# Computing the norm factors as a power of -0.5 on GpSimd, in one encoder layer kernel

## The chip, the cores and the metric

The kernel runs on one core of a Trainium2 chip. The core has five engines that run their own queues of instructions and meet by semaphores: TensorE (PE, with its weight loads PEld), VectorE (DVE), ScalarE (ACT), GpSimd (POOL) and SyncE (SP), which issues the transfers between memory and the on-chip buffers. The metric is the time of one execution on the device, in microseconds (us); the kernel before takes 1599.53 us as the median of three runs (1599.46 to 1602.58).

## The reference, cut to what matters

The model is one encoder layer on two sequences (a prompt and a sample) of 512 tokens with width 1024, each with a memory of 256 rows. All arithmetic is in 32-bit floats. The part that matters here is the norm:

```python
def _rmsnorm(x, g):
    xf = x.astype(jnp.float32)
    y = xf * lax.rsqrt(jnp.mean(xf * xf, axis=-1, keepdims=True) + EPS)
    return (y * g.astype(jnp.float32)).astype(x.dtype)
```

It is used on the input of the layer, on the memory, on the output of each of the four differential attention heads, on the input of the feed-forward part, and on the final output:

```python
    xn = _rmsnorm(x, p['norm_mix'][l])
    mn = _rmsnorm(mem, p['norm_mem'][l])
    h = xn @ p['w_in'][l]
    ...
    merged = term if merged is None else merged + term
    x = x + merged @ p['w_out'][l]
    xn2 = _rmsnorm(x, p['norm_ffn'][l])
    gate, up = jnp.split(xn2 @ p['w_ffn_in'][l], 2, axis=-1)
    return x + (jax.nn.silu(gate) * up) @ p['w_ffn_out'][l]
```

Between them lie a state space branch (S5) with a scan over the tokens, a differential attention of four heads, a cross attention to the memory, and gates that merge the three branches. Their functions on ScalarE are exponentials (softmax), hyperbolic tangents (the gates, GELU and SiLU) and squares.

## The kernel before

Activations are kept transposed: 128 features on the partitions, 512 tokens of a sequence along the free dimension. A product is a chain of matmuls with 128x128 weights and 512 columns that adds up in a bank of PSUM. To hold 32-bit precision each operand is split into a high and a low part (`split`, lines 134 and 135: ScalarE rounds, VectorE subtracts), and each product takes three matmuls (`mm3`). So TensorE has the most work of the engines.

The stages follow each other: norm of the inputs and memory products (to about 50 us of the profile), the S5 branch with gate products set between (to about 360 us), cross attention (to about 490 us), differential attention (to about 770 us), merging and the output projection (to about 940 us), the first feed-forward product in a form with seven products in place of eight (to about 1345 us), the second one, and the final norm.

A norm goes through one helper, `factor`. It gets the sums of squares of a sequence with tokens on the partitions, in a tile of 128x4 (`ss`, in PSUM or SBUF). ScalarE takes the root of the mean plus epsilon (line 198, Sqrt with scale and bias), VectorE the reciprocal (line 199), and then four transposes on TensorE with a broadcast operand (through line 69) spread the factors over all partitions, in a bank of PSUM named `bktr`, of which there are two to four. Later instructions of VectorE multiply the data with that bank. The calls are these, sixteen in all:

- two for the input (`ss0`, `ss1`), and one for the memory, all in the first 360 us;
- eight in `normed`, one for each head and sequence of the differential attention, with a bias of zero, since epsilon is added to the sums at line 896 already;
- two through `rstd` for the norm ahead of the feed-forward part, in the first round of its loop (`i == 0`);
- three in `final`, at the end of the kernel.

What sets the order: all instructions of an engine run in the order of its queue. In most of the kernel that order is made by a planner, which lays out the instructions by its own estimate of their durations (`schedule_with_timeline_sim=True`) and follows the order of the program where it has no reason to differ. `issue_after` puts instructions behind a named one on the same engine. In the cross attention, the differential attention, the last round of the first feed-forward product and nearly all of the second one, `PE.on = True` keeps TensorE's instructions in the order of the program; the other engines are planned there too. There `fill(n)` writes n matmuls of other work from a queue between the parts of the attention, so that TensorE has something to do while the other engines work. The loop of the differential attention handles one tile of 128 queries a step; `squares` of a head and sequence stands at the end of one step and `normed` at the end of the next, with two `fill(10)` and the transposes of the softmax between:

```python
        fill(10)
        if 1 < i <= n + 1 and steps[i - 2][2] == 3:
            squares(i - 2)
        if i > 2 and steps[i - 3][2] == 3:
            normed(i - 3)
```

GpSimd works in this kernel on adds and multiplies of SBUF tiles: the rotary embedding of queries and keys (lines 755 and 756), sums of weights (lines 454 to 457, 1023 to 1026), sums of squares (line 182), and products of the feed-forward part (line 1166).

Of the kernel before, what the change touches and what calls it, by code (L numbers as in the profile page):

```python
# [10 lines left out]
F32 = mybir.dt.float32  # L11
F32R = mybir.dt.float32r
I32 = mybir.dt.int32
AF = mybir.ActivationFunctionType
ALU = mybir.AluOpType
# [4 lines left out]
P = 128  # L20
L = 512
DM = 1024
# [3 lines left out]
EPS = 1e-6  # L26
# [46 lines left out]
def encoder(ctx: ExitStack, tc: tile.TileContext, a, out):  # L73
    nc = tc.nc
    V, S, PO, PE = nc.vector, nc.scalar, nc.gpsimd, InOrder(tc, nc.tensor)
# [3 lines left out]
    cst = ctx.enter_context(tc.tile_pool(name="cst", bufs=1))  # L79
# [32 lines left out]
    def aux():  # L112
        return bank("tr")
# [4 lines left out]
    nc.sync.dma_start(vec, a["vecs"])  # L118
    onec = cst.tile([P, 2], F32, name="onec")
    V.memset(onec, 1.0)  # L120
    V.memset(cst.tile([P, 8], F32, name="pad_l"), 0.0)
    epsc = cst.tile([P, 1], F32, name="epsc")
    S.activation(out=epsc, in_=onec[:, 0:1], func=AF.Sqrt)
    S.activation(out=epsc, in_=onec[:, 0:1], func=AF.Copy, scale=EPS)
# [1 line left out]
    def vcol(name, i=0):  # L126
        o = VEC[name][0] + i
        return vec[:, o : o + 1]
# [55 lines left out]
    def new_acc():  # L184
        return rp.tile([P, L], F32, tag="acc", name="acc", bufs=2)

    def rstd(acc, n, nt=4):


        ss = aux()  # L190
        for t in range(nt):
            PE.matmul(ss[:, t : t + 1], acc[:, t * P : (t + 1) * P], onec[:, 0:1], start=(t == 0), stop=(t == nt - 1))
        return factor(ss, n, nt)

    def factor(ss, n, nt=4, bias=epsc):

        rs = rp.tile([P, 4], F32, tag="rs", name="rs", bufs=4)
        S.activation(out=rs[:, :nt], in_=ss[:, :nt], func=AF.Sqrt, scale=1.0 / n, bias=bias)
        V.reciprocal(rs[:, :nt], rs[:, :nt])
        bc = aux()  # L200
        for t in range(nt):
            PE.transpose(bc[:, t * P : (t + 1) * P], rs[:, t : t + 1].broadcast_to([P, P]), ident)
        return rs, bc
# [26 lines left out]
    def sums(src, tag="wb", ss=None, ts=range(4)):  # L230

        nonlocal last_sq
        if ss is None:
            ss = rp.tile([P, 4], F32, tag="ss", name="ss", bufs=3)
        for t in ts:
            tk = slot(tag, [P, DM], name="tk")
            nc.sync.dma_start(tk, src[t])
            last_sq = S.activation(out=tk, in_=tk, func=AF.Square, accum_out=ss[:, t : t + 1])
        return ss
# [90 lines left out]
    with queued():  # L330
        x_load(0, range(3))
    norm = []
    mem_k(2, mw[2], lambda: norm.append(factor(ss0, DM)[1]))
    mw.append(weight(a["w_mv"][0]))
    with queued():
# [14 lines left out]
    with yielding(last_s):  # L350
        x_norm(0, norm[0], range(5, 8))
        _, bc = factor(ss1, DM)
# [163 lines left out]
    with behind():  # L516
# [3 lines left out]
        rs_, bc = factor(sums(a["memN"], "ld"), DM)  # L520
# [170 lines left out]
    for i in range(-AHEAD, len(steps) + 1):  # L691
        if i + AHEAD < len(steps):
            h, s, lt = steps[i + AHEAD]
# [12 lines left out]
        if 0 <= i < len(steps):  # L706
            h, s, lt = steps[i]
# [8 lines left out]
        if i > 0 and steps[i - 1][2] == 3:  # L716
            h, s, _ = steps[i - 1]
# [112 lines left out]
    s0, ss, osb = {}, {}, {}  # L830
# [66 lines left out]

    def normed(i):
        h, s, _ = steps[i]
        _, bc = factor(ss[h, s], P, bias=0.0)  # L900
        V.scalar_tensor_tensor(out=osb[h, s], in0=osb[h, s], scalar=g04, in1=bc, op0=ALU.mult, op1=ALU.mult)
        nc.sync.dma_start(bD[1, h, :, s * L : (s + 1) * L], osb[h, s])

    n = len(steps)
    for i in range(-1, n + 3):
        if i % 2 and i + 1 < n:
            scores(i + 1)
        if i == 22:
            queue.insert(1, first_in())
        fill(10 if i < n - 1 else 16)  # L910
        if 0 <= i < n:
            turn(i)
        if 0 < i <= n and steps[i - 1][2] % 2:
            outputs(i - 1)
# [5 lines that stand above are left out]
# [215 lines left out]
    for i in range(KFF):  # L1135
# [16 lines left out]
        if i == 0:  # L1152
            for s in range(NS):
                _, bc = rstd(accs[s], DM)
# [159 lines left out]
    def final(ss, c0, n, ready=(), late=()):  # L1314

        cs = slice(c0, c0 + n)
        _, bc = factor(ss, DM, n // P)
        if ready:
            b_ = new_acc()
            S.copy(b_[:, :n], bc[:, :n])  # L1320
        for m in (0, 1, 4, 5, 6, 7, 2, 3) if late else range(KD):
            if m in ready:
                PO.tensor_tensor(out=y[m][:, cs], in0=y[m][:, cs], in1=b_[:, :n], op=ALU.mult)
            else:
                with ExitStack() as es_:
                    if m in late:
                        es_.enter_context(tc.issue_after(last_add.ins))
                    V.scalar_tensor_tensor(out=y[m][:, cs], in0=y[m][:, cs], scalar=vcol("norm_final", m), in1=bc[:, :n],
                                           op0=ALU.mult, op1=ALU.mult)
            if m % 2 == 1:  # L1330
                nc.sync.dma_start(out[c0 // L, :, m - 1 : m + 1, c0 % L : c0 % L + n], y2[m // 2][:, :, cs])
            yield

    for c, n in ((0, L), (L, L // 2), (L + L // 2, L // 2)):
        acc = new_acc()
        for m in range(KD):
# [19 lines left out]
            if m == KD - 3:  # L1356
                ss = aux()
# [7 lines left out]

        ready = range(4, KD) if c == L else range(3) if c > L else ()
        end = final(ss if c + n == NT else column_sums(acc, n), c, n, ready, (2, 3) if c == L else ())
        if c != L:
            for _ in end:
# [423 lines left out]
```

## Time and profile before

| | |
|---|---|
| median of three runs | 1599.53 us |
| the profiled execution | 1599.28 us |
| its span, first to last instruction | 1597.5 us |
| TensorE busy | 1579.1 us (99%) |
| VectorE busy | 1163.7 us (73%) |
| ScalarE busy | 636.8 us (40%) |
| GpSimd busy | 542.6 us (34%) |
| granted TensorE clock, mean | 0.998 |

All durations come from one profiled execution. "Busy" counts the time in which at least one instruction of the engine runs. A view by groups gives for each line of the kernel, engine and operation the number of instructions, the sum and the mean of their durations, and the idle time of the engine just ahead of them with what ended it. The timeline gives one row for an instruction or a run of like ones: start, duration, engine, line, operation, what is written and read. Matmuls overlap, so a matmul of 512 columns shows a duration of 0.39 us while the next one starts 0.23 us after it.

### The profile page before, as it was taken

The page shows a single profiled execution, that of the slowest core. Times are in us where ns is not written, and L with a number is a line of the kernel's source. Part 1 is how long each engine was busy: PE and PEld are TensorE (multiplying, and loading weights), DVE is VectorE, ACT ScalarE, POOL GpSimd, SP SyncE. Part 2 cuts the span into 40 slices and gives each one's busy share as a digit, 9 for nine tenths or more (in the row PEclk, how much of TensorE's full clock was granted, in tenths as well). Part 3 has the DMA queues.
Part 4 walks back from the last instruction along what each step waited for, and adds up shares of the span by engine and source line. Part 5 has one row for each costly group of instructions (what it writes and reads, how often), then busy time and mean ns, then how long its engine had stood idle before and what let it go on. Part 6 is the DMA issues. An engine that isn't in the chain of part 4 may idle for free.

```text
span 1597.5 us, 21606 instructions
## 1 busy us (share of the span) xinstructions
PE 1579.1 (99%) x7838; PEld 1314.8 (82%) x7838; DVE 1163.7 (73%) x1856; ACT 636.8 (40%) x1140; POOL 542.6 (34%) x449
## 2 busy tenths in 40 slices
PE   9999999999999999999999999999999999999997
PEld 7888788888898789878878878888888888788877
DVE  7976997067774776775365578888898778998654
ACT  6544313265552465573123443323333224233323
POOL 0010100001333220300443366666665553444553
PEclk9999999999999999999999999999999999999999
DMA  9544523676762111253454432333332223985222
GB/s 366 174 159 152 175 94 123 182 261 213 262 224 102 46 55 40 73 178 133 138 190 140 144 108 89 123 122 129 119 116 109 81 91 115 355 332 196 75 67 106
DMA packets 104890, 237.84 MB, mean 149 GB/s; under 512 B 13520, under 2 KB 45008, under 8 KB 104784
## 3 DMA queue, kind: packets, MB, share of 16 engines
q1 hardware_dynamic: 104784, 236.47, 43.4%
q8 instruction: 61, 1.00, 0.2%
q14 instruction: 45, 0.37, 0.1%
HBM read 165.16 MB, written 71.27 MB: 148 GB/s over the span
## 4 chain that ended last, share of the span: by engine, by line
PE 89%; DVE 5%; issue 2%; DMA 2%; POOL 1%; ACT 1%; SPq 0%; POOLq 0%; DVEq 0%; ACTq 0%
PE bkmm L66 78%; PE bktr L66 3%; DVE tl L135 2%; PE bkoo L66 2%; PE bktr L69 2%; PE bksc L66 1%; PE bktr L1627 1%; PE bktr L1598 1%; PE bktr L1688 0%; PE bktr L1686 0%; PE bktr L1687 0%; PE bktr L1566 0%; DMA acc<-in_w_fo 0%; DMA mt<-in_memT 0%; DMA fl<-aD 0%
## 5 line engine op out<-in xcount | busy, mean ns | idle before, releaser
L66 PE MATMUL bkmm<-xh,wh 128*128 128x512 f32 x640 | 254.7, 398 | 0.0
L66 PE MATMUL bkmm<-xh,wl 128*128 128x512 f32 x640 | 251.1, 393 | 0.0
L66 PE MATMUL bkmm<-xl,wh 128*128 128x512 f32 x640 | 250.5, 391 | 0.0
L66 PE MATMUL bkmm<-tl,wh 128*128 128x512 f32 (+1 forms) x621 | 241.3, 389 | 1.4 <-DVE tl L135 1.4
L66 PE MATMUL bkmm<-th,wl 128*128 128x512 f32 (+1 forms) x621 | 241.1, 389 | 1.0 <-DVE wl L135 1.0
L66 PE MATMUL bkmm<-th,wh 128*128 128x512 f32 (+1 forms) x621 | 241.3, 389 | 0.0
L134 ACT CAST wh<-wf 128x1024 fp32r<-128x1024 f32 (+1 forms) x134 | 117.9, 880 | 220.8 <-PE bkmm L66 183.2
L135 DVE TENSOR_TENSOR wl<-wf,wh 128x1024 fp32r<-128x1024 f32 (+1 forms) x134 | 146.5, 1093 | 48.8 <-ACT wh L134 33.5
L66 PE MATMUL bkmm<-th,w 128*128 128x512 f32 x432 | 141.4, 392 | 3.5 <-DVE up L1102 2.0
L66 PEld LDWEIGHTS bkmm<-xh,wl 128*128 128x128 f32 x640 | 120.2, 188 | 26.6 <-issue 1.3
L66 PEld LDWEIGHTS bkmm<-xh,wh 128*128 128x128 f32 x640 | 120.4, 188 | 26.4 <-issue 3.4
L66 PEld LDWEIGHTS bkmm<-xl,wh 128*128 128x128 f32 x640 | 120.5, 188 | 22.6 <-issue 0.4
L66 PEld LDWEIGHTS bkmm<-tl,wh 128*128 128x128 f32 x621 | 116.6, 188 | 26.2 <-DVE tl L135 2.1
L66 PEld LDWEIGHTS bkmm<-th,wl 128*128 128x128 f32 x621 | 116.6, 188 | 25.6 <-DVE wl L135 1.9
L66 PEld LDWEIGHTS bkmm<-th,wh 128*128 128x128 f32 x621 | 116.6, 188 | 23.7
L1166 POOL TENSOR_TENSOR up<-up,acc 128x512 f32<-128x512 f32 x44 | 84.2, 1931 | 87.4 <-DVE up L1102 87.4
L454 POOL TENSOR_TENSOR raw<-raw 128x128 f32<-128x128 f32 x28 | 15.2, 546 | 285.0 <-DVE nb L545 206.5
L66 PEld LDWEIGHTS bkmm<-th,w 128*128 128x128 f32 x432 | 80.9, 188 | 24.9 <-DVE up L1102 4.5
L793 POOL TENSOR_TENSOR mg<-mg,gl 128x1024 f32<-128x1024 f32 x16 | 43.5, 2720 | 138.1 <-DVE gl L789 138.1
L66 PE MATMUL bkmm<-tl,w 128*128 128x512 f32 x216 | 84.2, 390 | 0.0
L66 PE MATMUL bkmm<-yh,wh 128*128 128x512 f32 x192 | 75.9, 397 | 0.8 <-DVE gl L789 0.8
L1165 ACT ACTIVATE ac<-gf 128x512 f32<-128x512 f32 x44 | 27.8, 633 | 122.5 <-DVE gf L1164 63.5
(651 smaller groups left out, 3580.8 us busy)
## 6 DMA issues: line engine op xcount, KB each, us to landing
wf<-in_w_in SPq DMA_DIRECT2D x40, 512.0 KB, 4.1
wD<-hl SPq DMA_DIRECT2D x28, 512.0 KB, 2.9
w<-wD SPq DMA_DIRECT2D x28, 512.0 KB, 4.8
gD<-gt SPq DMA_DIRECT2D x24, 512.0 KB, 2.8
gl<-gD SPq DMA_DIRECT2D x24, 512.0 KB, 3.4
wf<-in_w_fg SPq DMA_DIRECT2D x22, 512.0 KB, 3.7
wf<-in_w_fu SPq DMA_DIRECT2D x22, 512.0 KB, 3.6
aD<-ac SPq DMA_DIRECT2D x22, 512.0 KB, 3.0
```

The costliest lines, as they stand in the source:

```text
L66: return self.put(self.eng.matmul(*args, **kw))
L69: return self.put(self.eng.transpose(*args, **kw))
L134: h = S.copy(hi, src)
L135: l_ = V.tensor_tensor(out=lo, in0=src, in1=hi.bitcast(F32), op=ALU.subtract)
L454: PO.tensor_tensor(out=a22, in0=a21, in1=a22, op=ALU.add)
L793: PO.tensor_tensor(out=mg[m], in0=mg[m], in1=gt, op=ALU.add)
L1165: last_t = S.activation(out=ac[:, cs], in_=gf, func=AF.Tanh, scale=0.5)
L1166: PO.tensor_tensor(out=up, in0=up, in1=accs[s], op=ALU.mult)
L1598: PE.matmul(kp[64 * hf : 64 * hf + 48, g * 144 : (g + 1) * 144], l_[:, 2 * hf + g, :], o_[:, 4 * g4 + 2 * hf + g, :], start=(l_ is lr48), ...
L1627: PE.matmul(ps[:, g * P : (g + 1) * P], w_[:, gg * P : (gg + 1) * P], u_[:, 8 * o + gg, :], start=True, stop=True)
```

## The change

Thirteen of the sixteen factors are computed in another way. VectorE computes mean plus epsilon from the sums (multiply and add with two constants, one instruction), and GpSimd raises the result to the power of -0.5, by a tensor-tensor operation whose second operand is a tile filled with -0.5. ScalarE has no part in them. The three calls in `final` keep the root and the reciprocal. The tile of -0.5 takes the place of a padding tile of the same size, which was set to zero.

```diff
-    V.memset(cst.tile([P, 8], F32, name="pad_l"), 0.0)
+    half = cst.tile([P, 8], F32, name="half")
+    V.memset(half, -0.5)
...
-    def factor(ss, n, nt=4, bias=epsc):
+    def factor(ss, n, nt=4, eps=EPS, root=False):
 
         rs = rp.tile([P, 4], F32, tag="rs", name="rs", bufs=4)
-        S.activation(out=rs[:, :nt], in_=ss[:, :nt], func=AF.Sqrt, scale=1.0 / n, bias=bias)
-        V.reciprocal(rs[:, :nt], rs[:, :nt])
+        if root:
+            S.activation(out=rs[:, :nt], in_=ss[:, :nt], func=AF.Sqrt, scale=1.0 / n, bias=epsc)
+            V.reciprocal(rs[:, :nt], rs[:, :nt])
+        else:
+            V.tensor_scalar(out=rs[:, :nt], in0=ss[:, :nt], scalar1=1.0 / n, scalar2=eps, op0=ALU.mult, op1=ALU.add)
+            PO.tensor_tensor(out=rs[:, :nt], in0=rs[:, :nt], in1=half[:, :nt], op=ALU.pow)
...
     def normed(i):
         h, s, _ = steps[i]
-        _, bc = factor(ss[h, s], P, bias=0.0)
+        _, bc = factor(ss[h, s], P, eps=0.0)
...
     def final(ss, c0, n, ready=(), late=()):
 
         cs = slice(c0, c0 + n)
-        _, bc = factor(ss, DM, n // P)
+        _, bc = factor(ss, DM, n // P, root=True)
```

## The prediction

> **What bounds the kernel now.** I read the first page first: the busy times and the chain of work that ended last.
>
> ```profile
> span 1597.5 us, 21606 instructions
> PE 1579.1 (99%) x7838; PEld 1314.8 (82%) x7838; DVE 1163.7 (73%) x1856; ACT 636.8 (40%) x1140; POOL 542.6 (34%) x449
> PE 89%; DVE 5%; issue 2%; DMA 2%; POOL 1%; ACT 1%; SPq 0%; POOLq 0%; DVEq 0%; ACTq 0%
> ```
>
> TensorE is busy for all but 1597.5 - 1579.1 = 18.4 us, and it is 89% of the chain; ScalarE, which the edit relieves, is 1%. The edit leaves TensorE's work as it is, so it can take away at most idle time of TensorE, and lose time only where it makes TensorE wait. The second view is the busy time in stretches of 40 us, for where that idle time lies (columns: stretch, its length, then busy us and count for PE, PEld, DVE, ACT, POOL; then clock, DMA share, GB/s).
>
> ```profile
> 0.00:40.00 40.00, 37.32 (x166) 30.50 (x167) 31.25 (x127) 27.23 (x46) 0.66 (x6) 1.00 0.96 366
> ...
> 680.00:720.00 40.00, 39.20 (x220) 31.52 (x219) 30.19 (x52) 28.41 (x58) 0.00 (x0) 1.00 0.57 187
> ...
> 800.00:840.00 40.00, 39.39 (x173) 32.48 (x174) 24.53 (x29) 11.88 (x15) 18.86 (x7) 1.00 0.57 197
> 920.00:960.00 40.00, 38.60 (x179) 31.59 (x178) 30.32 (x30) 20.54 (x26) 28.73 (x22) 1.00 0.36 114
> 960.00:1000.00 40.00, 40.00 (x179) 32.86 (x178) 34.88 (x39) 13.93 (x19) 26.99 (x22) 1.00 0.22 80
> ...
> 1560.00:1600.00 40.00, 29.28 (x237) 28.54 (x236) 17.41 (x40) 13.04 (x31) 13.53 (x18) 0.90 0.29 105
> ```
>
> At the start 2.7 us are idle (the first transfers), in the middle 0.80 + 0.61 + 1.40 = 2.8 us, and in the last 37.5 us 8.2; the rest, 18.4 - 2.7 - 2.8 - 8.2 = 4.7 us, lies in stretches not shown, nearly all of it in the second feed-forward product. All thirteen changed factors come before 970 us. So what they can give back directly lies in the 2.8 us of the middle, under 0.2% of the time, which is about what a measurement of this kernel can tell from no change.
>
> **What is removed.** Next come the groups by line, for the root, the reciprocal and the loads of function tables on ScalarE.
>
> ```profile
> L198 ACT ACT_TABLE_LOAD x10 | 12.8, 1283 | 0.2
> L548 ACT ACT_TABLE_LOAD x5 | 6.4, 1283 | 0.1
> L1165 ACT ACT_TABLE_LOAD x2 | 2.6, 1283 | 0.0
> L123 ACT ACT_TABLE_LOAD x1 | 1.3, 1283 | 0.7 <-PEq L1786 0.7
> L410 ACT ACT_TABLE_LOAD x1 | 1.3, 1283 | 0.0
> L529 ACT ACT_TABLE_LOAD x1 | 1.3, 1283 | 0.0
> L632 ACT ACT_TABLE_LOAD x1 | 1.3, 1283 | 0.0
> L198 ACT ACTIVATE rs<-ss x8: 205/206/207, 571.4 to 762.6; 128x4 f32<-128x4 f32 x8
> L199 DVE RECIPROCAL rs<-rs x16: 164/177/179, 21.7 to 1589.9; 128x4 f32<-128x4 f32 x14, 128x2 f32<-128x2 f32 x2
> ```
>
> There are 21 loads of 1.283 us, each where ScalarE changes between the root and another function. An exponential and a tanh follow each other without one, starting 0.67 us apart, with no room for a load between:
>
> ```profile
> 702.45 0.70 ACT L548 ACTIVATE e<-bksc,nb 128x512 f32<-128x512 f32 x1
> ...
> 703.12 0.60 ACT L632 ACTIVATE gt<-bkmm 128x512 f32<-128x512 f32 x1
> ```
>
> So after the change three should be left: the one at line 123, one at the first tanh, and one ahead of the last norm. ScalarE loses 18 x 1.283 = 23.1 us of loads and thirteen roots of 0.2 to 0.3 us, some 26 us in all of its 636.8. I cost this gain at nothing, as TensorE is what ends last and none of its waits in the middle stands on a load. Two of them show it:
>
> ```profile
> 716.04 0.74 DVE L901 SCALAR_TENSOR_TENSOR osb<-osb,g,bktr 128x512 f32<-128x512 f32 x1
> 716.83 0.66 PE L69 MATMUL bktr<-ident,e 128*128 128x128 f32 x4 [0.77 <-DVE osb L901]
> 953.41 0.50 PE L66 MATMUL bkmm<-tl,wh 128*128 128x512 f32 x1 [0.60 <-DVE tl L135]
> ```
>
> The first waits for a bank that VectorE reads late, the other for VectorE's low parts of the feed-forward operands. The thirteen reciprocals of 0.18 us give way to thirteen multiply-adds on 128x4; the nearest row is line 896's 0.16 us on a tile of that size (below). VectorE's time stays, within 13 x 0.02 = 0.3 us. The memset of the padding tile only writes another number, in the same place.
>
> **What is added.** GpSimd gets thirteen powers of 128x4. No row shows a power. The low end is an add: in the rows below one of 512 columns takes 1.28 us and one of 128 takes 0.46, so 2.1 ns a column and 0.18 us fixed, and 4 columns would take 0.19 us. The high end is the dearest kind of GpSimd instruction on the page:
>
> ```profile
> L793 POOL TENSOR_TENSOR mg<-mg,gl 128x1024 f32<-128x1024 f32 x16 | 43.5, 2720 | 138.1 <-DVE gl L789 138.1
> ```
>
> A power is longer for each element than an add, but there are only 4 to a partition, so I take 0.5 us, near the 0.46 of the smallest add and 2.5 times the end of 0.19; both ends, 0.19 and 2.7 us, are kept for the range.
>
> The path of a factor was root, reciprocal, transposes; now it is multiply-add, power, transposes. Whether TensorE notices is a matter of slack: from the sums being there (line 896) to the transposes in TensorE's order (line 69). For the attention's eight norms TensorE keeps the order of the program, so a late power stops it. The first and the last of the eight, and then the two that have other work of GpSimd in the way:
>
> ```profile
> 569.63 0.16 DVE L896 TENSOR_TENSOR ss<-ss,s 128x4 f32<-128x4 f32 x1 [0.30 <-ACT acc L893]
> 573.50 0.60 PE L69 MATMUL bktr<-ident,rs 128*128 128x128 f32 x4
> ...
> 762.37 0.16 DVE L896 TENSOR_TENSOR ss<-ss,s 128x4 f32<-128x4 f32 x1 [0.32 <-ACT acc L893]
> 766.50 0.60 PE L69 MATMUL bktr<-ident,rs 128*128 128x128 f32 x4
> ...
> 596.87 1.28 POOL L755 TENSOR_TENSOR t<-t,rs 128x512 f32<-128x512 f32 x1 [8.15 <-DVE ss L896]
> 598.23 1.29 POOL L756 TENSOR_TENSOR t<-t,t 128x512 f32<-128x512 f32 x1
> 600.55 0.60 PE L69 MATMUL bktr<-ident,rs 128*128 128x128 f32 x4
> ...
> 652.92 1.26 DVE L896 TENSOR_TENSOR ss<-ss,s 128x4 f32<-128x4 f32 x1
> 654.24 1.30 POOL L756 TENSOR_TENSOR t<-t,t 128x512 f32<-128x512 f32 x1
> 656.80 0.60 PE L69 MATMUL bktr<-ident,rs 128*128 128x128 f32 x4
> ```
>
> With 0.18 us for the multiply-add, the first has 573.50 - 569.79 - 0.18 = 3.5 us for the power, the last 766.50 - 762.53 - 0.18 = 3.8; they stand for the six that meet no other work. In the second a power queued behind lines 755 and 756 starts at 599.52 and has 1.0 us; in the fourth it starts at 655.54 and has 1.3. So a power of 0.5 us costs TensorE nothing anywhere, one of 2.7 us costs 1.7 + 1.4 = 3.1 us. What hides it is the matmuls that `fill` puts between; without them the whole path would show, 0.7 us eight times. What waits in GpSimd's queue behind a power are the rotary instructions, 0.5 us later; the heads that they make come many steps later.
>
> The first norm of the input, and the second norm ahead of the feed-forward part:
>
> ```profile
> 21.65 0.18 DVE L199 RECIPROCAL rs<-rs 128x4 f32<-128x4 f32 x1 [0.46 <-ACT rs L198]
> 24.94 0.60 PE L69 MATMUL bktr<-ident,rs 128*128 128x128 f32 x4
> ...
> 962.68 0.17 DVE L199 RECIPROCAL rs<-rs 128x4 f32<-128x4 f32 x1
> 963.03 0.46 POOL L456 TENSOR_TENSOR raw<-raw 128x128 f32<-128x128 f32 x1
> 965.54 0.60 PE L69 MATMUL bktr<-ident,rs 128*128 128x128 f32 x4
> ```
>
> If the multiply-add stands where the reciprocal stood, the powers have 3.1 us and, after the one add in the way, 2.0 us. The three factors left (second input norm, memory, first sequence ahead of the feed-forward part) have their transposes some way behind the reciprocal too, and I cost them alike, at nothing. VectorE's L896 above shows one more effect: in the fourth norm 1.26 us beside GpSimd's work in place of 0.16. A power may stretch a VectorE instruction in that way, by up to its own length. That matters only around 945 us, where TensorE waits for VectorE soon after: 0 to 0.5 us. The Trainium skill (GPSIMD Engine Reference, section "Key points") has the same: GpSimd shares its SBUF interfaces with VectorE and contends with VectorE's instructions that read two SBUF inputs. The trace agrees with it by those two durations; by that rule the sum would be 0.5 us more, without it nothing.
>
> **Sum.** Loads 0, multiply-adds 0, power 0 (at 0.5 us), stretched VectorE 0 to 0.5 us: 1599.28 us of the profiled execution stay 1599.3 to 1599.8. The profiled execution lies 0.25 us under the median of 1599.53, so I say 1599.5 us.
>
> **Rivals.** First, the slower one: the power is long, computed element by element. It decides from about 2.7 us on, where the second and fourth norm alone give 3.1 us (0.2%). At 5 us they give 4.0 + 3.7, and the six others, by the two shown, 1.5 and 1.2, about 1.35 each, together 15.8 us: 1615 us. For it speaks that nothing here bounds a power; against it that the four columns are few.
>
> Second, the planner: it lays out the queues by its own durations, and these change in thirteen places. Outside the ordered stretches even TensorE's order may come out differently. TensorE has little left to lose in idle time (18.4 us), so a new order is rather worse than better: 3 to 10 us of new waits, 1603 to 1609. Against it: the stretch from 960 us on, with two of the norms just ahead, has TensorE busy for all of 40.00 us, so there is cover.
>
> Third, faster: relieved ScalarE, or a luckier order, takes waits away. All 2.8 us of the middle would give 1596.7, still within 0.2%; with half of the 4.7 us of the second feed-forward product too, 1594.3. For it speaks that table loads of 1.283 us stand in ScalarE's queue between softmax parts; against it that the waits shown are VectorE's.
>
> Fourth, the code of the power is fetched at its first use. The first such add on GpSimd in the trace:
>
> ```profile
> 387.14 0.82 POOL L454 TENSOR_TENSOR raw<-raw 128x128 f32<-128x128 f32 x1 [203.87 <-DVE nb L545]
> ```
>
> It is only 0.36 us longer than the 0.46 of the later one above, which the 3.1 us of the first norm would hide. To be felt it needs over 3.1 us there; at twice that slack, 6.2 us, 1599.5 + 3.1 = 1602.6. The Trainium skill (GPSIMD Engine Reference, section "Instruction dispatch") says that the first call to a freshly loaded kernel pays about 6 us for its code. By that rule the time would be an estimated 1602.4; the trace bears it out by no more than the 0.36 us, and no run here shows a power's code being loaded.
>
> That the change doesn't do what it says is small: if more loads than three stay, ScalarE only keeps what costs nothing now.
>
> **How the numbers follow.** No change within 0.2% (1596.3 to 1602.7): 0.45, its own range 1597.5 to 1602. Long power 0.17, worse order 0.13, fetched code 0.05 (just at the bound, counted as slower), faster 0.20. Together faster 0.20, same 0.45, slower 0.35. The range from 1595.5 to 1607 leaves out the better half of the faster case below it and the long powers above it, under 0.2 together.
>
> **What would show it.** Right: three table loads on ScalarE, no root before 1560 us, thirteen short GpSimd instructions at the power's line, the transposes of the norms without a wait for GpSimd, TensorE idle for about 18 us. Wrong: powers of over 2.7 us with TensorE's line 69 waiting for them, or new waits of TensorE at places that have no norm, which would be the planner's order.

## The result and the profile after

The changed kernel takes 1603.03 us (median of 15 runs, 1602.23 to 1606.98), the kernel before 1600.33 us (median of 15, 1599.22 to 1604.58). The ratio is 1.0018, with a 95% interval of 1.0011 to 1.0025: slower by 0.18%, or 2.7 us between the medians. The forecast was no change at 1599.5 us. The time lies inside the widest range of the prediction (1595.5 to 1607 us), but above both the band that it called "no change" (1596.3 to 1602.7) and that case's own range (1597.5 to 1602). The ratio is within 0.2%, yet clear of 1 by more than its uncertainty, where no loss was forecast. So what has to be explained is 2.7 us in 1600.

The first page of the profile after, with the group of the powers:

```profile
span 1601.1 us, 21614 instructions
PE 1580.2 (99%) x7838; PEld 1315.2 (82%) x7838; DVE 1163.9 (73%) x1856; ACT 612.8 (38%) x1109; POOL 560.7 (35%) x462
PE 84%; DVE 5%; DMA 3%; issue 3%; POOL 3%; ACT 1%; SPq 0%; POOLq 0%; DVEq 0%; ACTq 0%
L204 POOL TENSOR_TENSOR rs<-rs,half 128x4 f32<-128x4 f32 x13 | 18.4, 1418 | 333.3 <-DVE rs L203 312.4 <-DMA mD<-mf 20.9
```

ScalarE has 24.0 us less to do (636.8 before), as intended, and GpSimd 18.1 us more (542.6 before), which is the thirteen powers. TensorE does the same matmuls, but it is idle for 1601.1 - 1580.2 = 20.9 us in place of 18.4, and GpSimd's share of the chain has gone from 1% to 3%. The other 1.1 us by which this span is longer than the one before is in TensorE's busy time, whose ends are modelled. It can't be put down to the change, since a variant below (both norms back on the root) shows 1580.1 us of it in a span of 1597.8.

The table loads that are left on ScalarE, from the groups by line:

```profile
L124 ACT ACT_TABLE_LOAD x1 | 1.3, 1283 | 0.7 <-PEq L1791 0.7
L415 ACT ACT_TABLE_LOAD x1 | 1.3, 1283 | 0.0
L200 ACT ACT_TABLE_LOAD x1 | 1.3, 1283 | 0.0
```

There are three, the ones that the prediction named, so 18 loads are gone. What TensorE waits for in the changed kernel, by the sum over the span (total us, times, longest):

```profile
PE bktr L69 <- POOL rs L204: 2.5, 2, 1.6
PE bkmm L66 <- DVE tl L136: 1.4, 2, 0.8
```

The first row is new: among the waits of the kernel before there is none for GpSimd at the transposes of a norm. The stretches of 40 us say where the two waits are. Before, TensorE was busy for all of the stretch from 960 us (shown in the prediction) and for all of the one from 40 us:

```profile
40.00:80.00 40.00, 40.00 (x187) 33.03 (x186) 38.05 (x50) 23.76 (x52) 0.34 (x1) 1.00 0.50 174
```

After:

```profile
40.00:80.00 40.00, 39.04 (x182) 31.97 (x181) 36.87 (x50) 23.45 (x51) 5.27 (x2) 1.00 0.49 172
...
960.00:1000.00 40.00, 38.42 (x172) 31.53 (x171) 33.85 (x40) 11.45 (x16) 29.26 (x26) 1.00 0.23 81
```

The new idle time is 0.96 us in the first of these stretches and 1.58 us in the second, 2.54 us together: the 2.5 us by which TensorE's idle time has grown. The first is the second norm of the input, the other the second norm ahead of the feed-forward part.

**At 48 us the power itself is long.** The timeline of the changed kernel there:

```profile
43.28 0.17 DVE L203 TENSOR_SCALAR rs<-ss 128x4 f32<-128x4 f32 x1
43.35 3.10 DVE L259 TENSOR_TENSOR xl<-xt,xh 128x512 fp32r<-128x512 f32 x5
46.36 1.22 DVE L136 TENSOR_TENSOR wl<-wf,wh 128x1024 fp32r<-128x1024 f32 x1
43.53 4.93 POOL L204 TENSOR_TENSOR rs<-rs,half 128x4 f32<-128x4 f32 x1 [20.87 <-DMA mD<-mf]
48.51 0.65 PE L69 MATMUL bktr<-ident,rs 128*128 128x128 f32 x4 [0.96 <-POOL rs L204]
```

VectorE computes the mean (line 203), and goes straight on with six subtractions whose two operands are in SBUF (the on-chip buffer; PSUM is the other one, which the matmuls write), each beginning before the last one has ended, until 47.58. GpSimd's power of 128x4 starts at 43.53, beside them, and ends 0.88 us after the last of them, at 48.46. TensorE has run out of matmuls 0.96 us ahead of the transposes.

**At 968 us the power is short, but late in its queue:**

```profile
963.52 0.91 POOL L462 TENSOR_TENSOR raw<-raw 128x128 f32<-128x128 f32 x1
964.39 0.90 POOL L460 TENSOR_TENSOR raw<-raw 128x128 f32<-128x128 f32 x1
...
966.50 1.85 POOL L462 TENSOR_TENSOR raw<-raw 128x128 f32<-128x128 f32 x2
968.32 1.02 POOL L204 TENSOR_TENSOR rs<-rs,half 128x4 f32<-128x4 f32 x1
969.39 0.65 PE L69 MATMUL bktr<-ident,rs 128*128 128x128 f32 x4 [1.58 <-POOL rs L204]
964.02 0.15 DVE L203 TENSOR_SCALAR rs<-bktr 128x4 f32<-128x4 f32 x1
```

VectorE has the mean ready at 964.17. In GpSimd's queue the planner has put the power behind all the sums of raw weights of the next pieces: the add that is running and six more, 4.15 us until the power begins.

At the eleven other norms TensorE does not wait for the power. The first of all, and the fourth norm of the heads, for which the prediction had read 1.3 us:

```profile
21.63 1.03 POOL L204 TENSOR_TENSOR rs<-rs,half 128x4 f32<-128x4 f32 x1 [20.45 <-DVE rs L203]
...
25.00 0.60 PE L69 MATMUL bktr<-ident,rs 128*128 128x128 f32 x4
...
656.85 1.01 POOL L204 TENSOR_TENSOR rs<-rs,half 128x4 f32<-128x4 f32 x1
...
658.15 0.60 PE L69 MATMUL bktr<-ident,rs 128*128 128x128 f32 x4
```

### The profile page after: what moved, and what is told of

Its sections match the earlier page's. It is cut to its first block, busy times and chain, and to the rows that moved or that the text cites. A ratio compares the mean times of both kernels' runs of the same rounds, so it can differ in the third digit from the quotient of the medians.

```text
span 1601.1 us, 21614 instructions
## 1 busy us (share of the span) xinstructions
PE 1580.2 (99%) x7838; PEld 1315.2 (82%) x7838; DVE 1163.9 (73%) x1856; ACT 612.8 (38%) x1109; POOL 560.7 (35%) x462
## 3 DMA queue, kind: packets, MB, share of 16 engines
q8 instruction: 62, 1.02, 0.3%
## 4 chain that ended last, share of the span: by engine, by line
PE 84%; DVE 5%; DMA 3%; issue 3%; POOL 3%; ACT 1%; SPq 0%; POOLq 0%; DVEq 0%; ACTq 0%
PE bkmm L66 73%; PE bktr L66 2%; PE bkoo L66 2%; PE bktr L69 2%; DVE tl L136 1%; PE bksc L66 1%; PE bktr L1632 1%; DMA yt<-bD 1%; POOL mg L798 1%; PE bktr L1603 1%; DMA wf<-in_w_mv 0%; PE bktr L1693 0%; PE bktr L1692 0%; PE bktr L1691 0%; PE bktr L1571 0%
## 5 line engine op out<-in xcount | busy, mean ns | idle before, releaser
L204 POOL TENSOR_TENSOR rs<-rs,half 128x4 f32<-128x4 f32 x13 | 18.4, 1418 | 333.3 <-DVE rs L203 312.4
L66 PE MATMUL bkmm<-yl,wh 128*128 128x512 f32 x192 | 74.9, 390 | 0.0
L135 ACT CAST wh<-ws 128x1024 fp32r<-128x1024 f32 x44 | 46.2, 1050 | 72.9 <-PE bkmm L66 47.8
```

Source lines behind the costliest of these rows:

```text
L66: return self.put(self.eng.matmul(*args, **kw))
L135: h = S.copy(hi, src)
L204: PO.tensor_tensor(out=rs[:, :nt], in0=rs[:, :nt], in1=half[:, :nt], op=ALU.pow)
```

## The experiments

The theory after reading the two traces: the two waits are the whole loss, and the rest of the change gives and takes nothing. Rivals: a smaller loss or a gain from the relieved ScalarE is hidden in the 2.7 us too, and at 48 us the long power comes from its own code or data rather than from VectorE.

**The power alone and beside bursts of VectorE (p1_powers).** A probe times powers and adds on GpSimd, each behind one small instruction of VectorE, alone and then with a burst of VectorE's instructions directly behind.

```diff
+    r = t_("r" + name, 64)
+    V.tensor_scalar(out=r, in0=s, scalar1=0.5, scalar2=1.0, op0=ALU.mult, op1=ALU.add)
+    PO.tensor_tensor(out=r[:, :n], in0=r[:, :n], in1=half[:, :n], op=op)
+    # ... the burst, here k subtractions
+    V.tensor_tensor(out=o[:, :L], in0=a[:, :L], in1=b[:, :L], op=ALU.subtract)
```

> A probe that does none of the model's work and writes zeros. GpSimd raises tiles of 128x4 to the power of -0.5, first with VectorE idle, then while VectorE subtracts tiles back to back: 4, 8 and 16 times 128x512 with both operands in SBUF, 8 times 128x1024, 24 times 128x128, 8 times with one operand in PSUM, 8 times a 128x1024 multiply by a constant; and an add of 128x4 beside the first of these. Theory 'lock-out' (VectorE's instructions with two SBUF operands keep GpSimd out until a gap comes): alone 1.0 us; beside 4, 8 and 16 subtractions of 0.65 us about 3.5, 6 and 11 us, that is the length of the burst plus 0.9; beside the PSUM operand 1.0 us; the add of 128x4 lengthened as well. Theory 'turns' (each pass of the power over its data waits for the running VectorE instruction): the same 4 to 5 us beside 8 and beside 16, about twice that beside the tiles of 1024 columns, and under 2 us beside 128 columns. Theory 'code' (the 4.9 us are a fetch of the power's code): the first power or the second is about 5 us long with VectorE idle, and no later one is longer than 1.1 us by more than one VectorE instruction.

Powers of 4, 4, 1 and 64 columns, then adds of 4 and 64 columns, and a power of 4 columns beside sixteen subtractions of 512 columns:

```profile
5.88 1.01 POOL L24 TENSOR_TENSOR ral<-ral,half 128x4 f32<-128x4 f32 x1 [5.44 <-DVE ral L24]
7.20 1.01 POOL L24 TENSOR_TENSOR ral<-ral,half 128x4 f32<-128x4 f32 x1 [0.31 <-DVE ral L24]
8.52 0.55 POOL L24 TENSOR_TENSOR ral<-ral,half 128x1 f32<-128x1 f32 x1 [0.31 <-DVE ral L24]
...
12.60 10.55 POOL L24 TENSOR_TENSOR ral<-ral,half 128x64 f32<-128x64 f32 x1 [0.31 <-DVE ral L24]
23.45 0.20 POOL L24 TENSOR_TENSOR rad<-rad,half 128x4 f32<-128x4 f32 x1 [0.31 <-DVE rad L24]
23.96 0.32 POOL L24 TENSOR_TENSOR rad<-rad,half 128x64 f32<-128x64 f32 x1 [0.31 <-DVE rad L24]
...
33.29 1.41 POOL L24 TENSOR_TENSOR rtt<-rtt,half 128x4 f32<-128x4 f32 x1 [4.40 <-DVE rtt L24]
```

A power of 128x4 takes 1.01 us, the first as long as the second, which speaks against theory 'code'. Beside the burst of sixteen it took 1.41, far from 4.93, and the longest of all, beside eight subtractions of 1024 columns, took 1.94: neither of the two other theories came out as foretold. Here every subtraction wrote the same tile, and the records show each beginning 0.034 us after the end of the one before; in the kernel they overlap. So this probe did not settle where the 4.93 us come from.

**One norm back to root and reciprocal, then the other, then both.** The flag `root` that the change already has for the last norm is set for the second input norm, for the second feed-forward norm, and for both.

```diff
-        _, bc = factor(ss1, DM)
+        _, bc = factor(ss1, DM, root=True)          # e1 and e3
...
-                _, bc = rstd(accs[s], DM)
+                _, bc = rstd(accs[s], DM, root=s == 1)   # e2 and e3
```

> The changed kernel, with the second input norm back on root and reciprocal. Theory 'two places' (the changed kernel loses 1.1 us at the second input norm and 1.6 us at the second norm ahead of the feed-forward part, and no more): 1.1 us less than the changed kernel, so 1.6 us over the kernel before, ratio 1.0010; no wait of TensorE near 48 us. Theory 'plan' (the loss comes from other places of the changed order, and waits in the first 50 us are made up later): the ratio stays at 1.0018.

> The changed kernel, with the second norm ahead of the feed-forward part back on root and reciprocal, which brings back two table loads there. Theory 'two places': 1.6 us less than the changed kernel, 1.1 us over the kernel before, ratio 1.0007. Theory 'plan': the ratio stays at 1.0018.

> Both of these norms back on root and reciprocal; eleven powers stay. Theory 'two places': the time of the kernel before within 0.5 us, ratio 1.0000, and the eleven other powers with their removed table loads give nothing either way. Theory 'plan': over 1.0010. A third, 'relief' (the removed table loads do give something, covered up by the two waits): under 0.9995.

Against the kernel before (1600.34 us), the first gave 1601.3 us, ratio 1.0007 (0.9998 to 1.0016); the second 1600.45, ratio 1.0002 (0.9993 to 1.0011); both together 1599.71, ratio 1.0001 (0.9992 to 1.001). Each of the first two keeps one wait of TensorE. With only the input norm undone:

```profile
PE bktr L69 <- POOL rs L204: 1.7, 1, 1.7
```

With only the feed-forward norm undone:

```profile
PE bktr L69 <- POOL rs L204: 1.0, 1, 1.0
```

With both undone there is no such row. The two waits add up to 1.7 + 1.0 = 2.7 us here, and to 2.5 us in the changed kernel, which lost 2.7. The times go the same way, both somewhat under what was expected (1.0010 and 1.0007), though an interval of 0.0009 to either side can't by itself tell 1 us from none. The third run is the one that says most: eleven powers, with 5 table loads left of 21, give 1.0001. Its interval and that of the change (from 1.0011) do not overlap. The relief of ScalarE is worth nothing that can be measured, and eleven of the powers cost nothing that can be measured either.

**Bursts of VectorE without gaps (p2_bursts).** The probe again, with a tile of its own for each subtraction, so that the subtractions overlap as in the kernel.

```diff
-    V.tensor_tensor(out=o[:, :L], in0=a[:, :L], in1=b[:, :L], op=ALU.subtract)
+    V.tensor_tensor(out=outs[i][:, :L], in0=a[:, :L], in1=b[:, :L], op=ALU.subtract)
```

> A second probe, which writes zeros again. In the first, each of VectorE's subtractions wrote the same tile and so waited for the one before, with 0.035 us between two of them, and the power beside them took 1.4 us, however long the burst; the 4.9 us did not come up. Here each writes a tile of its own, so that each starts before the one before has ended, as in the model's kernel near 44 us. Bursts of 2, 4, 8 and 16 subtractions of 128x512 in SBUF, 8 of 128x1024, 16 of 128x128, 8 with one operand in PSUM, 8 multiplies of 128x1024 by a constant, and an add of 128x4 beside 8. Theory 'lock-out' (an unbroken row of VectorE instructions with two SBUF operands keeps GpSimd out to its end): the power takes the rest of the burst and 0.9 us more: 2.0, 3.2, 5.6 and 10.4 us for 2, 4, 8 and 16, about 10 for the 1024 columns, 1.0 with the PSUM operand, and the add over 4 us. Theory 'code or data' (the length has nothing to do with VectorE): 1.0 to 1.4 us everywhere.

```profile
16.25 9.71 DVE L24 TENSOR_TENSOR o<-a,b 128x512 f32<-128x512 f32 x16
16.41 10.42 POOL L24 TENSOR_TENSOR rtt<-rtt,half 128x4 f32<-128x4 f32 x1 [3.53 <-DVE rtt L24]
...
40.64 1.01 POOL L24 TENSOR_TENSOR rttps<-rttps,half 128x4 f32<-128x4 f32 x1 [0.31 <-DVE rttps L24]
```

Beside sixteen subtractions the power of 128x4 took 10.42 us and ended 0.87 us after the burst (25.96): what the kernel shows at 48 us, longer. Beside eight subtractions that read one operand from PSUM it took 1.01. So the length does not come from the power's code or data. The add of 128x4, 0.20 us alone, took 4.79 beside eight. But beside 2, 4 and 8 subtractions the power took 1.4 us, and beside eight of 1024 columns 1.92, so the burst alone did not decide, and that part of the expectation failed.

**The same bursts several times (p3_repeats).** Only the list of bursts is changed: each is repeated, two to four times.

> A probe of its own that does none of the model's work: a power of 128x4 beside bursts of VectorE's subtractions, the same burst several times over, to see what decided in the probe before between 1.4 us (bursts of 2, 4 and 8 subtractions of 512 columns, and of 1024 columns) and 10.42 or 4.02 us (16 of 512, 16 of 128 columns). Theory 1, the burst alone decides: bursts of 16 subtractions of 512 columns give about 10.4 us every time, those of 4 and 8 and of 1024 columns 1.4 to 1.9 us every time, and sixteen of 128 columns 4.0 us every time. Theory 2, every burst can keep GpSimd out, and whether a power slips in is settled at its start: the same burst gives 1.4 us at one time and the burst's length (2.9 us for 4, 5.3 for 8, 10.4 for 16) at another. Theory 3, the place of the result tiles decides: the bursts of 16 written in the reverse order of the tiles give another time than those in order. Beside subtractions that read PSUM all theories say 1.0 us. An add beside sixteen subtractions: 9.6 us where it is kept out, 0.6 where not.

The powers beside the first two bursts of sixteen subtractions and the first two of eight, and the second of three adds beside sixteen (the number in brackets is how long GpSimd had been idle before):

```profile
7.21 1.39 POOL L24 TENSOR_TENSOR rtt<-rtt,half 128x4 f32<-128x4 f32 x1 [0.31 <-DVE rtt L24]
...
16.94 10.42 POOL L24 TENSOR_TENSOR rtt<-rtt,half 128x4 f32<-128x4 f32 x1 [8.35 <-DVE rtt L24]
...
48.12 1.39 POOL L24 TENSOR_TENSOR rtt<-rtt,half 128x4 f32<-128x4 f32 x1 [0.31 <-DVE rtt L24]
...
53.04 5.60 POOL L24 TENSOR_TENSOR rtt<-rtt,half 128x4 f32<-128x4 f32 x1 [3.53 <-DVE rtt L24]
...
167.39 9.61 POOL L24 TENSOR_TENSOR radd<-radd,half 128x4 f32<-128x4 f32 x1 [9.16 <-DVE radd L24]
```

The second theory holds for all but the bursts of four: the same burst gives 1.39 us at one time and its own length the next. Bursts of sixteen gave 1.39, 10.42, 1.38, 10.42 us, those of eight 1.39, 5.60, 1.39, 5.60; written to the tiles in reverse order, 1.39 and 10.42; of 1024 columns 9.87, 1.92, 9.87; sixteen of 128 columns 1.19, 4.02, 1.01; the bursts of four all let the power in, and two of three adds took 0.58 us. Beside PSUM operands the power took 1.01 us both times. The third theory falls, as the reverse order gives the same pair of times. So GpSimd either slips in near the start of the burst, or it is kept out until the burst is over. VectorE loses nothing either way: a burst of sixteen lasts 9.72 us with the power slipped in and 9.71 with it kept out.

What tips it, no run here shows, but the rows have a pattern. Of the 25 powers beside unbroken bursts with two SBUF operands in p2 and p3, the 15 before which GpSimd had been idle for 1.13 us or less all slipped in, and the 10 before which it had been idle for 2.15 us or more were all kept out; in the kernel the power of 4.93 us came after 20.87 idle. One add breaks the pattern: it slipped in (0.58 us) after 8.66 us idle, behind a burst that read PSUM. No run changed the idle time alone, so it is a hint and not a cause.

**The feed-forward norm's place in GpSimd's queue (e4_sums_behind).** All powers stay. Only the sums of raw weights of this place are put behind the power in GpSimd's queue.

```diff
-            PO.tensor_tensor(out=rs[:, :nt], in0=rs[:, :nt], in1=half[:, :nt], op=ALU.pow)
+            last_pow = PO.tensor_tensor(out=rs[:, :nt], in0=rs[:, :nt], in1=half[:, :nt], op=ALU.pow)
...
-            half_piece((last_t, last_sum))
+            half_piece((last_t, last_sum, last_pow))
```

> The changed kernel with all thirteen powers, where the sums of weight pieces on GpSimd in the feed-forward loop are issued behind the last power. Nothing else is moved by hand. Theory 'two places': the power near 964 us starts within 0.5 us of its operand, TensorE's 1.6 us wait near 968 us goes, and 1.1 us over the kernel before stay: ratio 1.0007. If the wait came from the power's own 1.0 us and not from the queue ahead of it, the ratio stays at 1.0018.

It took 1601.1 us against 1600.13 of the kernel before, ratio 1.0005 (0.9996 to 1.0014).

```profile
964.07 1.40 POOL L208 TENSOR_TENSOR rs<-rs,half 128x4 f32<-128x4 f32 x1 [7.10 <-DVE rs L207]
...
968.21 0.60 PE L69 MATMUL bktr<-ident,rs 128*128 128x128 f32 x4
```

The power takes 1.40 us here, longer than the 1.02 in the changed kernel, but it is done at 965.47, and the transposes come at 968.21 without a wait: it was its place in the queue, and not its own length, that cost 1.6 us. The wait at 48 us, 1.0 us, is still there.

**Both places in order (e5_both_orders).** In addition the second input norm's factor is written ahead of the subtractions, where VectorE's next instructions read a bank of PSUM.

```diff
+        _, bc = factor(ss1, DM)
         x_norm(0, norm[0], range(5, 8))
-        _, bc = factor(ss1, DM)
```

> As the one before, and the second input norm's factor is written ahead of the last three normalised tiles of the first sequence, so that VectorE's multiply-add stands three PSUM-reading instructions (2.1 us) earlier. Theory 'lock-out': the power then runs beside those, takes 1.0 to 1.5 us, and is ready near 42.5 us, so TensorE's 1.1 us wait near 48 us goes too: all thirteen powers at the time of the kernel before, ratio 1.0000. Theory 'code or data': the power still takes 4.9 us, but starts 2 us earlier, so it ends near 46.3 and the wait goes all the same; the power's duration tells the two apart.

It took 1599.71 us against 1600.13, ratio 0.9998 (0.9989 to 1.0007).

```profile
41.59 0.74 DVE L261 SCALAR_TENSOR_TENSOR xt<-xt,vec,bktr 128x512 f32<-128x512 f32 x1
...
41.76 1.01 POOL L208 TENSOR_TENSOR rs<-rs,half 128x4 f32<-128x4 f32 x1 [18.80 <-DVE rs L207]
...
47.68 0.60 PE L69 MATMUL bktr<-ident,rs 128*128 128x128 f32 x4
```

The same power takes 1.01 us, and no transposes of a norm wait for GpSimd any more. With all thirteen powers kept, the two places put right bring the kernel back to the time of before within the interval, and not measurably under it.

**The power twice in the heads' norms (e7_twice).** To see how much cover the eight norms of the heads have, the power is computed twice there, the first into a spare part of the tile of -0.5.

```diff
+            if eps == 0.0:
+                PO.tensor_tensor(out=half[:, 4 : 4 + nt], in0=rs[:, :nt], in1=half[:, :nt], op=ALU.pow)
```

> The changed kernel, with the power of each of the eight head norms computed twice, one behind the other on GpSimd (the first result is not used). It measures the cover that TensorE's other work gives. From the changed kernel's rows seven of the eight have 1.4 us or more between the end of the power and the transposes, and the fourth (power ends at 657.86, transposes at 658.15) has next to none: 0.8 to 1.0 us over the changed kernel, ratio 1.0023. Were the powers on the path of TensorE in all eight: 8 us, ratio 1.0068.

It took 1604.86 us, ratio to the kernel before 1.0031 (1.0019 to 1.0042).

```profile
PE bktr L69 <- POOL rs L206: 4.2, 4, 1.7
...
602.67 0.65 PE L69 MATMUL bktr<-ident,rs 128*128 128x128 f32 x4 [0.70 <-POOL rs L206]
```

There are two waits more than in the changed kernel, at the second and at the fourth of the eight, 0.70 and 0.89 us, where one, at the fourth, had been expected; the six others take a second power without a wait. At the second norm a rotary instruction of 1.29 us came between the two powers, so the delay there was more than one power's length. In the changed kernel the second norm's power had 601.80 - 599.36 = 2.4 us, as it ran between the two rotary instructions and not behind both (the prediction read 1.0), and the fourth's had 658.15 - 656.85 = 1.3, as read.

## Why the prediction was wrong, point by point

*What bounds the kernel, and what the relief is worth.* Right. Eighteen loads and thirteen roots less on ScalarE (24.0 us measured, "some 26" forecast) gave nothing that can be measured: 1.0001 in the run with eleven powers, which keeps five loads, and 0.9998 in the one with thirteen, each with 0.0009 to either side. The faster rival falls with that.

*The power's own price.* Taken as 0.5 us between 0.19 and 2.7; measured 1.01, inside the bounds and twice the value taken. In the heads' norms that made no difference, since even the tightest, the fourth, had 1.3 us. The rival of a long power needed 2.7 us of the power's own; the 4.93 us at 43.53 were not its own.

*Code fetched at the first use.* The first power of the kernel took 1.03 us and the first of the probe 1.01, as long as any other: no such cost. The 6 us that the Trainium skill gives for the first call to a freshly loaded kernel (GPSIMD Engine Reference, section "Instruction dispatch") do not show up here for this operation.

*The second input norm: the step that failed first.* "The three factors left ... I cost them alike, at nothing." No row was looked at for what runs beside the power. Before, this factor had 47.32 - 43.40 = 3.9 us between the reciprocal's end and the transposes, enough for a power of 1.01. The row that mattered was the one that followed the reciprocal on VectorE in the kernel before:

```profile
43.23 0.17 DVE L199 RECIPROCAL rs<-rs 128x4 f32<-128x4 f32 x1
43.32 3.06 DVE L254 TENSOR_TENSOR xl<-xt,xh 128x512 fp32r<-128x512 f32 x5
46.31 1.21 DVE L135 TENSOR_TENSOR wl<-wf,wh 128x1024 fp32r<-128x1024 f32 x1
...
47.32 0.60 PE L69 MATMUL bktr<-ident,rs 128*128 128x128 f32 x4
```

This is an unbroken burst to 47.52, of the kind that keeps GpSimd out; a power that ends 0.87 us later is at 48.39, which is 1.1 us past the transposes; the wait measured 0.96. The 0.87 was not known before the runs. But the burst ends 0.2 us past the transposes, so with the 0.5 us taken for the power, a power kept out until then could have been priced at 0.7 us. And the kernel before has a row that hints at such a hold, though what caused it there was not tested: a copy of line 1580 takes 4.25 us beside VectorE's instructions with two SBUF operands, where the three others of that line took 1.35 each:

```profile
174.91 4.25 POOL L1580 COPY cxi<-cn 128x128 f32<-128x128 f32 x1 [4.76 <-DVE cxr L1554]
```

The prediction weighed this contention in one direction alone, GpSimd stretching VectorE by 0 to 0.5 us, from the row of 1.26 us; the sum by the other direction was missing. The Trainium skill has that direction too (SBUF — State Buffer, section "Who interferes with whom"): of a VectorE instruction with two SBUF inputs and a GpSimd instruction that reads SBUF, the one that comes second is blocked entirely until the first is done. The trace agrees that it is blocked and not merely slowed: the power lasts 4.93 us for 1.01, and ends 0.88 us after the burst. The probes add that a row of overlapping VectorE instructions can keep the way closed through all of them (10.42 us beside sixteen), and that it does so only some of the times.

*The second feed-forward norm: the other step that failed.* "After the one add in the way, 2.0 us." It was the add that was running and six more, 4.15 us from the mean to the start of the power. In the kernel before, too, an add is running at the end of the reciprocal (962.85) and six more follow, past the transposes at 965.54, without a gap until 966.15 and with one of 0.08 us ahead of the last. After the first, which the prediction shows, these are:

```profile
963.46 0.46 POOL L455 TENSOR_TENSOR raw<-raw 128x128 f32<-128x128 f32 x1
963.88 0.87 POOL L457 TENSOR_TENSOR raw<-raw 128x128 f32<-128x128 f32 x2
964.72 1.43 POOL L456 TENSOR_TENSOR raw<-raw 128x128 f32<-128x128 f32 x1
966.23 0.46 POOL L457 TENSOR_TENSOR raw<-raw 128x128 f32<-128x128 f32 x1
```

A power in the gap at 966.15 would end at 966.15 + 1.01 = 967.16, 1.6 us too late, and one behind the last add at 966.69 + 1.01 = 967.70, 2.2 us too late. The 1.58 us measured lie at the lower end. In the changed kernel the power did stand behind the last add, but the whole order had shifted: the mean came 1.3 us later than the reciprocal had, and TensorE reached the transposes 2.3 us later. The prediction counted only the row next to the one that it quoted, and took for granted that the planner would fit the power in as early as it could. It should have stood as a bound: between the place behind the add that is running and the end of the row.

*The planner.* Half right: it was a choice of the planner that cost 1.6 us, but at the norm itself, not the 3 to 10 us of waits at other places. The argument against this rival, that the stretch from 960 us has TensorE busy all the time, was no argument: cover is what lies between two instructions, and a stretch that is full before the change says nothing about how late an operand may come.

*VectorE around 945 us.* The wait of TensorE for VectorE's low parts there is 1.4 us in both kernels: the power stretched nothing that mattered, so this term was nothing. The power itself was drawn out to 2.36 us there, with enough slack behind it.

## What to carry to other kernels

When a step moves to GpSimd, read what VectorE does right behind the instruction that feeds it: if that is an unbroken row of instructions with two SBUF operands, the small step may last until the row is over, so issue it where VectorE reads PSUM. Read GpSimd's queue to the end of its row of work and not to the next instruction: with a planner in between, the new instruction may come last in it. Relief of an engine that none of the waits of the busiest engine stands on was worth nothing here that could be measured (24.0 us of ScalarE), while each new hop between engines needs its slack checked place by place.

## What was not expected of the hardware

A power on GpSimd costs by the column: 0.55 us for 1, 1.01 for 4 and 10.55 for 64, about 0.16 us a column, where an add of 64 columns takes 0.32 us. And the contention with VectorE has two outcomes for the same instructions: 1.39 us or the whole burst (5.60 or 10.42 us), in turn through a row of repeats; even an add of 128x4, 0.20 us alone, took 0.58, 9.61 and 0.58 us in three of them.
